# An encoder kernel in split float32: the up projection of three FFNs in groups of seven block products, and part of the weight splitting handed to adding DMAs

## The chip, the cores and the metric

One core of a Trainium2 chip runs the whole program. The metric is device microseconds (us) of one execution; the time before is the median of 3 runs. A core has five engines that are used here. TensorE (PE in the profile) multiplies matrices, VectorE (DVE) and ScalarE (ACT) work elementwise, GpSimd (POOL) does little, and SyncE (SP) issues the DMAs that bring the weights. Each engine takes its instructions in a fixed order that a scheduler lays down when the kernel is built; they meet through semaphores.

## The reference

x has 256 tokens of 1024 features, everything is float32, and there are two layers. The part that matters here is the FFN, which stands twice in each layer, so four times in all:

```python
def swiglu(h, w_up, w_down):
    a, b = jnp.split(h @ w_up, 2, axis=-1)
    return (jax.nn.silu(a) * b) @ w_down

for l in range(DEPTH):
    h = rms_norm(x, ffn1_pre_g[l])
    x = x + 0.5 * rms_norm(swiglu(h, ffn1_w_up[l], ffn1_w_down[l]), ffn1_post_g[l])
    ...   # mixer: pooling, differential attention, cross-attention, gates, w_out
    h = rms_norm(x, ffn2_pre_g[l])
    x = x + 0.5 * rms_norm(swiglu(h, ffn2_w_up[l], ffn2_w_down[l]), ffn2_post_g[l])
```

w_up is 1024 x 5632 (2816 gate columns, then 2816 value columns), w_down is 2816 x 1024.

## The kernel before, in words

**Stages.** `stages` lists six in a row: FFN, mixer, FFN, FFN, mixer, FFN. Each ends with a sandwich norm (`post_norm`, then `pre_norm` of the next stage) for the two halves of 128 tokens, called c = 0 and c = 1. While the norm of c = 1 runs, PE already works on c = 0 of the next stage; the transposes of c = 1 (`late`) are placed behind the 37th matmul of that stage (`T_UP = 36`).

**Split float32.** A product of float32 operands is made of three matmuls in the PE's float32r format: high times high, high times low, low times high (`mm3`, L218). So each weight has to be split. Weights come in units of 1 MB (`raw`, 128 x 2048 float32), one DMA each from SP. `next_unit` (L105) splits a unit in two halves of 1024 columns (in four quarters for the first five units of a stage, `FINE`): ACT copies it, rounded, into `wh` (L116), DVE subtracts, raw - wh, into `wl` (L117). The pools hold 3 `raw` tiles and 5 pairs of `wh` and `wl`, and so the splitting runs at most five units ahead of PE.

**The up projection.** A pair p is 256 gate and 256 value columns with all 1024 rows of w_up, two units; an FFN has 11 pairs. In the first FFN, and for pairs 0 and 1 of the later three, `form_b2` (L253) makes a bank of 128 tokens by 512 columns for each c: 24 matmuls of 512 columns. `swiglu` (L327) takes the silu on ACT (L335) and the product on DVE (L336); `turn` (L338) transposes the 128 x 256 result on PE (L341) and splits it into `hid` (L156, L157). For pairs 2 to 10 of the later three FFNs, `up2` (L347) uses `form_a2` (L235), with the weights as the stationary operand: for each bank eight matmuls of 512 and eight of 256 columns, whose result stands already transposed; ACT and DVE add the parts (L356, L357), take silu and product (L358, L359), and split.

**The down projection.** `down(p)` (L298) splits one unit of w_down, 256 rows, and adds it into four accumulator banks, 24 matmuls of 512 columns (`rows_chunk`, L256). Down units 0 to 7 stand between the pairs, two behind; units 8 to 10 are done in `tail`.

**What sets the order.** The order of the program text, a pool's free buffers and the scheduler set the order on each engine; a few positions are pinned by hand (`issue_after`). PE's order follows the text closely. DVE and ACT serve two kinds of work from one queue: splits of units that come later, and what the current banks need (evictions, norms, splits of hid).

Of the kernel before, what the change touches and what calls it, by code (L numbers as in the profile page):

```python
# [35 lines left out]
T_SC = (242, 336)  # L36
T_KT = (200, 222)
# [10 lines left out]
def encoder_kernel(ctx, tc, x_d, xt_d, mem_d, memt_d, pos_d, w_d, gains_d, cols_d, lamv_d, poolw_d, cst_d, out_d):  # L48
# [4 lines left out]
    rawp = ctx.enter_context(tc.tile_pool(name="rawp", bufs=3))  # L53
# [3 lines left out]
    mixp = ctx.enter_context(tc.tile_pool(name="mixp", bufs=1))  # L57
    s4 = ctx.enter_context(tc.tile_pool(name="s4", bufs=2))
    s2 = ctx.enter_context(tc.tile_pool(name="s2", bufs=5))
# [45 lines left out]
    def next_unit():  # L105
        parts = 4 if fine[0] > 0 else 2
        fine[0] -= 1
        if not raws:
            load_unit()
        raw = raws.pop(0)  # L110
# [3 lines left out]
        for s in range(parts):  # L114
            cs = slice(s * n, (s + 1) * n)
            high = nc.scalar.copy(out=h[:, cs], in_=raw[:, cs])  # L116
            low = nc.vector.tensor_tensor(out=l[:, cs], in0=raw[:, cs], in1=h.bitcast(F32)[:, cs], op=ALU.subtract)  # L117
# [4 lines left out]
        return h, l  # L122

# [19 lines left out]
    def rstd_of(halves, fold=1.0, between=None, into=None, listed=False):  # L143
        s, sq = sm(2), []
        for i, h in enumerate(halves):
            junk = small.tile([P, 512], BF16, name="junk", bufs=2)
# [32 lines left out]
    def pre_norm(c, src, g, xx):  # L179
# [13 lines left out]
        def turn():  # L193
            tps = []
            for b in range(2):
# [5 lines left out]
                split(pv, xh[:, c, b * 4:b * 4 + 4, :], xl[:, c, b * 4:b * 4 + 4, :])  # L201
            return tps
# [83 lines left out]
    def ffn(i, xx, late, g_post, finish, ahead, raw_rstd=None):  # L286
# [4 lines left out]
        def hid_pair(p):  # L291
            hid[p] = (hids.tile([P, 2, 2, P], F32R, name="hid"), hids.tile([P, 2, 2, P], F32R, name="hid"))
            return hid[p]

        def lhs_of(c, kk, k):
            return hid[kk][0][:, c, k, :], hid[kk][1][:, c, k, :]

        def down(p):  # L298
            w = next_unit()
# [3 lines left out]
            for c in range(2):  # L303
                rows_chunk(c, acc[c], [(w, p)], lhs_of, 0, NPR - 1)

        pending = []

        def flush():
            while pending:
                pending.pop(0)()  # L310
# [7 lines left out]

        def up_first(p, ws):
            banks = [ma_bank(), ma_bank()]  # L320
            for i, w in enumerate(ws):
                for c in range(2):
                    mm3(banks[c], half_b(w, i, c, xx), i == 0, i == 1)
# [3 lines left out]
        def swiglu(p, c, ps):  # L327
            sg = t2((P, 2, P))
            gate, value = (ps[:, 256 * j:256 * j + 256].rearrange("p (u m) -> p u m", u=2) for j in range(2))
            hn = t2((P, 2, P))  # L330
            if raw_rstd:
# [601 lines left out]
```

## Time and profile before

| what | value |
|---|---|
| median of 3 runs | 1139.08 us (1138.89 to 1139.74) |
| the profiled execution | 1138.92 us, its span 1136.9 us |
| PE busy | 1127.8 us |
| DVE busy | 749.6 us |
| ACT busy | 626.8 us |
| POOL busy | 25.6 us |
| bytes moved by DMA | 218.32 MB |

The span runs from the first to the last instruction of the profiled execution. A busy share is that of an engine's instructions with matmul ends modelled: successive matmuls overlap in it. The mean duration of a matmul is therefore longer than the step from one to the next, and the step is what counts for a row of matmuls. The same holds, less strongly, for DVE and ACT. The chain of waits goes back from the last instruction to whatever released it, and gives the stretches of the program in order of time. The three later FFNs lie at 384 to 570, 570 to 756 and 946 to 1137 us of the span.

### The profile page before, as it was taken

Reading aid. Unit: us, or ns where it says so; the run is one execution under the profiler, and the core shown is the slowest. Engines: PE = TensorE matmul, PEld = TensorE weight load, DVE = VectorE, ACT = ScalarE, POOL = GpSimd, SP = SyncE. Lnnn points to the kernel's source line nnn. Section 1 sums busy time; section 2 is a strip of 40 time slices with the busy share of each in tenths; the row PEclk is TensorE's granted clock in tenths of the full one; section 3 lists DMA queues with packets and bytes.
Section 4 is the critical chain, followed back from the end, with each engine's and each line's share of the span. In section 5 each row is a group of like instructions: output and inputs, shape, how many; then the busy total and the mean of one; then the engine's idle time right before and its main releaser. Section 6 shows DMA issues by size and latency. Waiting matters only on the chain.

```text
span 1136.9 us, 14731 instructions
## 1 busy us (share of the span) xinstructions
PE 1127.8 (99%) x5679; PEld 943.7 (83%) x5679; DVE 749.6 (66%) x1164; ACT 626.8 (55%) x1121; POOL 25.6 (2%) x37
## 2 busy tenths in 40 slices
PE   9999999999999999999999999999999999999997
PEld 6888888888788888888888888888887888888886
DVE  6767456567758866566586756575676688666553
ACT  7666445456573565555565655555566546555541
POOL 0000000000000100000000000010000001000000
PEclk9999999999999999999999999999999999999999
DMA  8976553544554575555465655545455545655530
GB/s 318 340 239 229 194 189 131 213 171 148 205 183 168 204 256 192 186 185 186 148 238 206 222 189 184 186 158 204 161 180 184 203 148 177 249 185 185 186 111 37
DMA packets 35493, 218.32 MB, mean 192 GB/s; under 512 B 4192, under 2 KB 4448, under 8 KB 11232
## 3 DMA queue, kind: packets, MB, share of 16 engines
q1 hardware_dynamic: 35424, 217.40, 53.4%
q8 instruction: 44, 0.72, 0.2%
q14 instruction: 25, 0.20, 0.1%
HBM read 216.33 MB, written 1.05 MB: 191 GB/s over the span
## 4 chain that ended last, share of the span: by engine, by line
PE 97%; DMA 1%; ACT 1%; DVE 0%; POOL 0%; issue 0%; SPq 0%; DVEq 0%; POOLq 0%; ACTq 0%
PE ma L224 36%; PE acc L266 25%; PE mb L243 13%; PE ma L243 13%; PE mb L224 2%; PE acc L224 2%; PE mb L199 1%; PE acc L599 1%; PE mb L341 1%; PE acc L622 1%; PE mb L497 1%; PE acc L685 1%; DMA hid<-in_xt 1%; DMA raw<-in_w 0%; PE acc L669 0%; PE mb L758 0%
## 5 line engine op out<-in xcount | busy, mean ns | idle before, releaser
L117 DVE TENSOR_TENSOR wl<-raw,wh 128x1024 fp32r<-128x1024 f32 (+1 forms) x444 | 459.0, 1075 | 150.8 <-ACT wh L116 145.0
L116 ACT CAST wh<-raw 128x1024 fp32r<-128x1024 f32 (+1 forms) x444 | 391.3, 935 | 187.8 <-issue 99.9
L224 PE MATMUL ma<-wh,xhl 128*128 128x512 f32 x1184 | 376.6, 393 | 0.8 <-ACT wh L116 0.8
L224 PEld LDWEIGHTS ma<-wh,xhl 128*128 128x128 f32 x1184 | 221.4, 188 | 47.5 <-ACT wh L116 1.7
L224 PE MATMUL ma<-wl,xhl 128*128 128x512 f32 x592 | 233.6, 395 | 0.2 <-DVE wl L117 0.2
L266 PE MATMUL acc<-wh,hid 128*128 128x512 f32 x704 | 224.6, 391 | 0.0
L243 PE MATMUL ma<-xhl,wh 128*128 128x512 f32 x432 | 157.4, 398 | 0.0
L243 PE MATMUL mb<-xhl,wh 128*128 128x512 f32 x432 | 157.0, 397 | 0.0
L266 PEld LDWEIGHTS acc<-wh,hid 128*128 128x128 f32 x704 | 132.2, 188 | 26.2
L266 PE MATMUL acc<-wl,hid 128*128 128x512 f32 x352 | 137.1, 389 | 0.0
L224 PEld LDWEIGHTS ma<-wl,xhl 128*128 128x128 f32 x592 | 111.3, 188 | 23.9 <-DVE wl L117 1.2
L243 PE MATMUL mb<-xhl,wl 128*128 128x256 f32 x432 | 112.5, 281 | 0.0
L243 PE MATMUL ma<-xhl,wl 128*128 128x256 f32 x432 | 112.4, 281 | 0.0
L243 PEld LDWEIGHTS ma<-xhl,wh 128*128 128x128 f32 x432 | 81.2, 188 | 15.8
L243 PEld LDWEIGHTS mb<-xhl,wh 128*128 128x128 f32 x432 | 81.5, 189 | 14.5
L357 DVE TENSOR_TENSOR s<-mb,s 128x256 f32<-128x256 f32 x54 | 22.9, 424 | 103.8 <-ACT s L356 103.8
L243 PEld LDWEIGHTS mb<-xhl,wl 128*128 128x128 f32 x432 | 81.6, 189 | 5.0
L243 PEld LDWEIGHTS ma<-xhl,wl 128*128 128x128 f32 x432 | 81.5, 189 | 4.6
L266 PEld LDWEIGHTS acc<-wl,hid 128*128 128x128 f32 x352 | 66.2, 188 | 13.7
L356 ACT COPY s<-mb 128x256 f32<-128x256 f32 x54 | 20.2, 373 | 58.7 <-PE mb L243 58.7
L358 ACT ACTIVATE s<-s 128x256 f32<-128x256 f32 x54 | 22.6, 418 | 50.6 <-DVE s L357 50.6
L140 POOL TENSOR_TENSOR sm<-sm,mhalf 128x1 f32<-128x1 f32 (+1 forms) x26 | 22.6, 869 | 1024.5 <-DVE sm L149 845.6
(162 smaller groups left out, 966.0 us busy)
## 6 DMA issues: line engine op xcount, KB each, us to landing
raw<-in_w SPq DMA_DIRECT2D x189, 1024.0 KB, 4.8
gain<-in_gains SPq DMA_DIRECT2D x17, 512.0 KB, 5.1
raw<-in_w SPq DMA_DIRECT2D x8, 256.0 KB, 5.7
hid<-in_memt SPq DMA_DIRECT2D x8, 256.0 KB, 6.0
hid<-in_xt SPq DMA_DIRECT2D x4, 256.0 KB, 5.6
raw<-in_w SPq DMA_DIRECT2D x2, 512.0 KB, 6.9
x<-in_x SPq DMA_DIRECT2D x4, 256.0 KB, 6.6
hid<-in_mem SPq DMA_DIRECT2D x4, 256.0 KB, 6.1
```

What stands on the lines that cost most here:

```text
L116: high = nc.scalar.copy(out=h[:, cs], in_=raw[:, cs])
L117: low = nc.vector.tensor_tensor(out=l[:, cs], in0=raw[:, cs], in1=h.bitcast(F32)[:, cs], op=ALU.subtract)
L140: nc.gpsimd.tensor_tensor(out=r, in0=v, in1=mhalf[:, :n], op=ALU.pow)
L199: tps.append(nc.tensor.transpose(out=ps[:, k * P:(k + 1) * P], in_=xn[:, i * P:(i + 1) * P], identity=ident))
L224: done.append(nc.tensor.matmul(out=out, lhsT=lhsT, rhs=rhs, start=(first and i == 0), stop=(last and i == n - 1)))
L243: nc.tensor.matmul(out=o, lhsT=ww[:, k, ms], rhs=rhs, start=(k == 0 and o is full), stop=(k == KT - 1 and o is full))
L266: done.append(nc.tensor.matmul(out=banks[b], lhsT=a, rhs=ww[:, k, fs], start=(kk == first and k == 0 and i == 0), stop=(kk == last and k = ...
L341: nc.tensor.transpose(out=tp[:, u * P:(u + 1) * P], in_=hn[:, u, :], identity=ident)
L356: nc.scalar.copy(out=half, in_=banks[i][:, S:2 * S])
L357: nc.vector.tensor_tensor(out=half, in0=banks[i][:, 0:S], in1=half, op=ALU.add)
L358: nc.scalar.activation(out=t[:, 0:S], in_=t[:, 0:S], func=AF.Silu)
L497: ins.append(nc.tensor.transpose(out=tp[:, i * P:(i + 1) * P], in_=a[:, hh, kt * P:(kt + 1) * P], identity=ident))
```

## The change

**Seven products for eight.** In the later three FFNs, six of the 11 pairs are done two at a time. The 256 x 1024 input is seen as 2 x 2 blocks (c, and the halves of the 1024 features), the 1024 x 1024 piece of w_up of two pairs as 2 x 2 blocks (the same halves, and 512 gate or 512 value columns), one raw unit for each block. `group` makes the four result blocks of seven products of blocks, 12 matmuls of 512 columns each, in place of eight. To that end it adds raw units to each other on DVE before they are split (four additions of 128 x 2048 in a group), uses four sums of token blocks (`token_sums`, once in an FFN, from unsplit copies that `pre_norm` keeps with four ACT copies), and puts the products together with seven DVE additions of 128 x 512. The first group of an FFN (`s0`) also does pair 0 in the ordinary way, around the late transposes; pairs 1 and 2 are its group. The other groups (`g5`, `g9`) do pairs 5, 6 and 9, 10. Pairs 3, 4, 7 and 8 go by `form_b2`, so `form_a2` and `up2` are gone. `PLAN` is the order.

**Down units 0 to 7** of these FFNs get their low part without DVE: ACT writes -wh into `wl` (line 121 of the new kernel), and a DMA issued by POOL adds raw to it in memory (line 122), two halves of 512 KB a unit.

**Buffers.** 5 `raw` tiles for 3, 8 `s2` tiles for 5, one `junk` tile for two; the mixer's tiles `vc`, `up`, `pooled` and `pw` live in one raw tile. In all FFNs the transposes of a pair now are made in `down`, behind its c = 0 and c = 1 parts.

```diff
+PLAN = [[(t[0], int(t[1:])) for t in plan.split()] for plan in (
+    "u2 d0 u3 d1 u4 d2 u5 d3 u6 d4 u7 d5 u8 d6 u9 d7 u10",
+    "s0 d0 u3 d1 u4 d2 g5 d3 d4 u7 d5 u8 d6 g9 d7",
+)]
...
-    rawp = ctx.enter_context(tc.tile_pool(name="rawp", bufs=3))
+    rawp = ctx.enter_context(tc.tile_pool(name="rawp", bufs=5))
...
             high = nc.scalar.copy(out=h[:, cs], in_=raw[:, cs])
+            if added:
+                nc.scalar.activation(out=l[:, cs], in_=h.bitcast(F32)[:, cs], func=AF.Copy, scale=-1.0)
+                nc.gpsimd.dma_start(out=l[:, cs], in_=raw.bitcast(F32R)[:, cs], accum_op=ALU.add)
+                continue
             low = nc.vector.tensor_tensor(out=l[:, cs], in0=raw[:, cs], in1=h.bitcast(F32)[:, cs], op=ALU.subtract)
...
+                if keep is not None:
+                    keep[c, b] = t2()
+                    nc.scalar.copy(out=keep[c, b], in_=ps)
...
         def down(p):
-            w = next_unit()
+            w = split_unit(next_raw(), 2, True) if kept else next_unit()
...
             for c in range(2):
                 rows_chunk(c, acc[c], [(w, p)], lhs_of, 0, NPR - 1)
+                flush(1 - c)
...
+        def token_sums():
+            a11, a12, a21, a22 = (kept[c, b] for c in range(2) for b in range(2))
+            s1 = t2()
+            nc.vector.tensor_tensor(out=s1, in0=a22, in1=a21, op=ALU.subtract)
+            nc.vector.tensor_tensor(out=a21, in0=a11, in1=a21, op=ALU.subtract)
+            nc.vector.scalar_tensor_tensor(out=a11, in0=s1, scalar=-1.0, in1=a11, op0=ALU.mult, op1=ALU.subtract)
+            nc.vector.scalar_tensor_tensor(out=a12, in0=a11, scalar=-1.0, in1=a12, op0=ALU.mult, op1=ALU.subtract)
+            for j, t in enumerate((s1, a11, a21, a12)):
+                split(t.rearrange("p (k t) -> p k t", t=P), sums[:, 0, 4 * j:4 * j + 4, :], sums[:, 1, 4 * j:4 * j + 4, :])
+
+        def group(p, start):
+            def turn(c, value, gate):
+                nc.scalar.activation(out=gate, in_=gate, func=AF.Silu)
+                nc.vector.scalar_tensor_tensor(out=value, in0=value, scalar=-1.0, in1=gate, op0=ALU.mult, op1=ALU.mult)
+                turned(value, c, [p, p + 1])
+
+            if start:
+                ws = (next_unit(), next_unit())
+                done = up(p, 0, ws, acc_bank)
+                w11, w21 = next_raw(), next_raw()
+                a, e = ma_bank(), ma_bank()
+                done += product(a, tokens(0, 0), split_unit(w11, 2))
+                done += product(e, tokens(0, 1), split_unit(w21, 2))
+                issue_after(late, done[T_UP])
+                s, g0 = t2(), t2()
+                nc.scalar.copy(out=s, in_=a)
+                add(g0, s, e)
+                up(p, 1, ws, acc_bank)
+                p += 1
+                token_sums()
+                w12, w22 = next_raw(), next_raw()
+            else:
+                w11, w12, w22, w21 = (next_raw() for _ in range(4))
+                a = ma_bank()
+                product(a, tokens(0, 0), split_unit(w11, 2))
+                flush()
+                s = t2()
+                nc.scalar.copy(out=s, in_=a)
+            add(w11, w11, w12)
+            d = mb_bank()
+            product(d, summed(0), split_unit(w11, 2))
+            flush()
+            add(w11, w11, w22)
+            add(w12, w12, w22)
+            b = mb_bank()
+            product(b, summed(1), split_unit(w11, 2))
+            u2, u3 = t2(), t2()
+            add(u2, s, b)
+            c = ma_bank()
+            product(c, summed(2), split_unit(w12, 2))
+            add(u3, u2, c)
+            add(u2, u2, d)
+            if not start:
+                e, g0 = ma_bank(), s
+                product(e, tokens(0, 1), split_unit(w21, 2))
+                add(g0, s, e)
+            v1 = t2()
+            add(v1, u3, d)
+            add(w21, w21, w11)
+            g = ma_bank()
+            if start:
+                product(g, tokens(1, 1), split_unit(w21, 2))
+                add(u3, u3, g)
+                turn(1, v1, u3)
+            f = mb_bank()
+            product(f, summed(3), split_unit(w22, 2))
+            add(u2, u2, f)
+            turn(0, u2, g0)
+            if not start:
+                product(g, tokens(1, 1), split_unit(w21, 2))
+                add(u3, u3, g)
+                turn(1, v1, u3)
```

**How the instructions move.** First place: DVE at the start of the second FFN (384 us of the span before), from the scaling of c = 1 in the norm on. Before, there are splits of units (`wl`), the split of the late transposes (`xhl`), the swiglu products (L336) and splits of `hid`:

```order
L191 TENSOR_SCALAR s4_3305<-s4_3305,sm_3315 128x512 x2
L117 TENSOR_TENSOR wl_3374<-raw_3371,wh_3373 128x512 x3
L336 TENSOR_TENSOR s2_3413<-ma_3387,s2_3412 128x256
L117 TENSOR_TENSOR wl_3523<-raw_3520,wh_3522 128x512 x2
L157 TENSOR_TENSOR xhl_3209<-mb_3319,xhl_3209 128x512
L157 TENSOR_TENSOR xhl_3209<-mb_3326,xhl_3209 128x512
L117 TENSOR_TENSOR wl_3523<-raw_3520,wh_3522 128x512 x2
L336 TENSOR_TENSOR s2_3447<-ma_3416,s2_3446 128x256
L157 TENSOR_TENSOR hid_3384<-mb_3441,hid_3383 128x256
```

Now, at the same place (line numbers are those of the new kernel: L124 is the split of a unit, L368 an addition, L345 the swiglu product, L169 any other split, L379 to L382 the token sums, with the splits of the sums among them):

```order
L203 TENSOR_SCALAR s4_3303<-s4_3303,sm_3313 128x512 x2
L124 TENSOR_TENSOR wl_3416<-raw_3393,wh_3415 128x1024
L368 TENSOR_TENSOR raw_3391<-raw_3391,raw_3486 128x2048
L169 TENSOR_TENSOR xhl_3203<-mb_3317,xhl_3203 128x512
L169 TENSOR_TENSOR xhl_3203<-mb_3326,xhl_3203 128x512
L124 TENSOR_TENSOR wl_3493<-raw_3391,wh_3492 128x1024
L345 TENSOR_TENSOR s2_3388<-acc_3362,s2_3387 128x256
L368 TENSOR_TENSOR raw_3486<-raw_3486,raw_3488 128x2048
L368 TENSOR_TENSOR s2_3434<-s2_3433,ma_3396 128x512
L124 TENSOR_TENSOR wl_3493<-raw_3391,wh_3492 128x1024
L345 TENSOR_TENSOR s2_3470<-acc_3437,s2_3469 128x256
L169 TENSOR_TENSOR hid_3466<-mb_3462,hid_3465 128x256
```

The additions of whole raw units stand in front of the split of the late transposes and among the evictions of pair 0; the four sums and their splits follow, then the splits of the four remaining products. From the row behind the scaling to the second half of the last product's `wl`, DVE now has 34 instructions: 11 half-unit splits, 4 additions of 2048 columns, 13 additions, subtractions or splits of 512, 2 fused ones of 512 and 4 of 256 columns.

Second place: ACT at the end of that first group. The casts of the last two products (`wh_3564`, `wh_3586`) stand in front of down unit 0 (`wh_3609`) and its negation:

```order
L119 CAST wh_3540<-raw_3486 128x1024
L119 CAST wh_3564<-raw_3393 128x1024 x2
L119 CAST wh_3586<-raw_3488 128x1024 x2
L119 CAST wh_3609<-raw_3607 128x1024 x2
L121 ACTIVATE wl_3610<-wh_3609 128x1024 x2
L388 ACTIVATE s2_3537<-s2_3537 128x512
```

POOL's queue, which held only the norms' square roots there, now has the two additions of each of the eight down units between those of one stage's end and the next:

```order
L152 TENSOR_TENSOR sm_3299<-sm_3295,mhalf_90 128x1
L152 TENSOR_TENSOR sm_3313<-sm_3309,mhalf_90 128x1
L122 DMA wl_3610<-raw_3607 128x1024 x2
L122 DMA wl_3759<-raw_3756 128x1024 x2
L122 DMA wl_3883<-raw_3880 128x1024 x2
```

So the low part of a down unit now goes raw, ACT, ACT, POOL, DMA, PE, where it went raw, ACT, DVE, PE.

More of the change, by code (lines that the diff above doesn't have):

```diff
@@ L819, in ahead @@
                     nx["mem"] = mem_gain(l)
-            late = ffn(i, cur, late, gain(l * 10 + row + 1), finish, ahead, [rst[:, c:c + 1] for c in range(2)] if i == 0 else None)
+            late = ffn(i, cur, late, kept, gain(l * 10 + row + 1), finish, ahead, [rst[:, c:c + 1] for c in range(2)] if i == 0 else None)
         else:
             late = mix(l, cur, late, mem, finish)
-        cur, mem = nx.get("xx"), nx.get("mem")
+        cur, mem, kept = nx.get("xx"), nx.get("mem"), nx.get("kept")
 def _constants(np):
```

179 lines of the change are left out of this document (93 added, 86 removed).

## The prediction

> **What bounds the kernel now.** I read the page first, then the chain of waits in order of time, then busy time by stage, then the groups with shapes kept apart, and last the timelines of single engines at a stage boundary. The page's engine table, its row of the granted clock, and the chain's shares:
>
> ```profile
> PE 1127.8 (99%) x5679; PEld 943.7 (83%) x5679; DVE 749.6 (66%) x1164; ACT 626.8 (55%) x1121; POOL 25.6 (2%) x37
> PEclk9999999999999999999999999999999999999999
> PE 97%; DMA 1%; ACT 1%; DVE 0%; POOL 0%; issue 0%; SPq 0%; DVEq 0%; POOLq 0%; ACTq 0%
> ```
>
> The chain runs through PE for 97% of the span, so PE's own work sets the time, and less of it is worth something as long as nobody else becomes late. The three later FFNs, by stage (window, length, then busy us and count of PE, PEld, DVE, ACT, POOL, then clock, DMA share, GB/s):
>
> ```profile
> 384.00:570.00 186.00, 186.00 (x962) 158.31 (x961) 120.92 (x181) 101.68 (x178) 3.50 (x4) 1.00 0.56 198
> 570.00:756.00 186.00, 186.00 (x962) 158.11 (x961) 123.51 (x189) 104.18 (x185) 3.43 (x4) 1.00 0.56 198
> ```
>
> PE has no gap there; DVE is busy 121 of 186 us (65%), so it has some 65 us to spare in an FFN, but spread over it. Steps come from the chain (start, length, engine, target, line, count), first in the first FFN, then in the second:
>
> ```profile
> 47.91 5.44 PE ma L224 x24
> 53.36 0.22 PE mb L341 x2
> 53.58 5.48 PE ma L224 x24
> 59.05 0.22 PE mb L341 x2
> 59.27 0.93 PE acc L266 x4
> ...
> 401.88 5.47 PE ma L224 x24
> ...
> 424.51 2.81 PE ma L243 x16
> 427.32 2.82 PE mb L243 x16
> 430.14 2.82 PE ma L243 x16
> 432.96 2.82 PE mb L243 x16
> 435.78 5.45 PE acc L266 x24
> 441.23 2.81 PE ma L243 x16
> ```
>
> 24 matmuls of 512 columns take 5.47 us, 0.228 each, and two transposes 0.22. A pair by `form_b2` with its four transposes takes 59.27 - 47.91 = 11.36 us; a pair by `form_a2` 435.78 - 424.51 = 11.27; a down unit 5.45.
>
> **What PE saves.** A group of two pairs is 7 x 12 = 84 matmuls and 8 transposes: 84 x 0.228 + 4 x 0.22 = 20.0 us. Before, an FFN's up projection is 2 x 11.36 + 9 x 11.27 = 124.2 us; after, 5 x 11.36 + 3 x 20.0 = 116.8. That is 7.4 us an FFN, 22.2 for three: seven products for eight give 2.7 us a group, and the pairs 3, 4, 7 and 8 lose 0.1 each. Against the profiled execution's 1138.9 us, PE's work alone would give 1116.7.
>
> **What DVE gets.** Durations by shape (mean ns after the comma) and, from DVE's timeline, steps between instructions that stand back to back:
>
> ```profile
> L117 DVE TENSOR_TENSOR wl<-raw,wh 128x1024 fp32r<-128x1024 f32 x324 | 383.0, 1220 | 139.9 <-ACT wh L116 134.3 <-issue 1.1 <-PE ma L224 0.4
> L752 DVE TENSOR_TENSOR hid<-hid 128x512 f32<-128x512 f32 x8 | 5.5, 686 | 0.1
> ```
> ```profile
> 380.84 4.29 DVE L117 TENSOR_TENSOR wl<-raw,wh 128x512 fp32r<-128x512 f32 x7
> 385.06 0.20 DVE L149 TENSOR_SCALAR sm<-sm 128x1 f32<-128x1 f32 x1
> 385.92 1.41 DVE L216 SCALAR_TENSOR_TENSOR x<-s,sm,x 128x512 f32<-128x512 f32 x2
> 390.31 0.88 DVE L191 TENSOR_SCALAR s<-s,sm 128x512 f32<-128x512 f32 x2 [0.45 <-POOL sm L140]
> 400.06 2.36 DVE L117 TENSOR_TENSOR wl<-raw,wh 128x1024 fp32r<-128x1024 f32 x2 [2.47 <-ACT wh L116]
> 402.34 0.42 DVE L336 TENSOR_TENSOR s<-ma,s 128x256 f32<-128x256 f32 x1
> 402.68 0.41 DVE L157 TENSOR_TENSOR hid<-mb,hid 128x256 fp32r<-128x256 f32 x1
> ```
>
> Steps: 1024 columns 2.36 - 1.22 = 1.14 us; 512 columns (4.29 - 0.69) / 6 = 0.60; a fused one of 512 1.41 - 0.75 = 0.66; 256 columns 402.68 - 402.34 = 0.34. No row has 2048 columns: going on from 512 to 1024 (0.54 per 512) gives 2.2, four pieces of 512 give 2.4, and a gain cannot be excluded from these rows, since two TENSOR_SCALARs of 512, at 390.31, take 0.88. I take 2.2, nearest to the two-input rows.
>
> The first group `s0` is the place where it decides. From the scaling of c = 1 to the second half of the last product's `wl`, DVE's queue holds (front, the order) 11 x 1.14 + 4 x 2.2 + 13 x 0.60 + 2 x 0.66 + 4 x 0.34 = 31.8 us. It cannot be begun earlier, since the queue is in order and the scaling ends the norm's chain; the unit buffers, five ahead of PE, are nearly all taken then. PE's rows at that place before:
>
> ```profile
> 384.03 0.39 PE L224 MATMUL ma<-wh,xhl 128*128 128x512 f32 x1
> 392.42 1.04 PE L199 MATMUL mb<-ident,s 128*128 128x128 f32 x8
> 393.21 0.48 PE L224 MATMUL ma<-wl,xhl 128*128 128x512 f32 x1
> ```
>
> Call 384.03 zero. The scaling ends at 7.2 (390.31 + 0.88), the late transposes start at 8.4 and take 0.8. Behind them PE has 11 matmuls (rest of product e), 24 (pair 0, c = 1), five products of 12, and 4 transposes: 95 x 0.228 + 0.8 + 0.44 = 22.9 us, so it would end the group at 31.3. DVE is done with the last `wl` at 7.2 + 31.8 = 39.0 at the earliest, and six matmuls (1.4) stand behind: 40.4. PE waits 9.1 us. Two things come on top: two half splits of product a, and the gain of one bank, now stand ahead of c = 1's variance in place of three quarters (2 x 1.14 + 0.60 - 3 x 0.60 = 1.1, 1.0 taken), and DVE waits about 0.4 for the cast that follows the first addition (0.95, below). **10.5 us a start group**, 31.5 for three, between 8.5 (the second one has a split less behind the scaling) and 12.3 (additions at 2.4, and 1 us of more such waits). PE waits where DVE's order puts it: before product d (the token sum s1 comes behind the additions and the evictions of pair 0), and before g and f.
>
> In `g5` and `g9` the splits run ahead of PE by up to five units, with little else on DVE during the pairs before. What stays behind the preceding down unit's end is the cast for e, then e, 2.28, a hid split 0.34, an addition 2.2, f 2.28, half of g 1.14, u2 0.60, the rest of g 1.14, u3, u2, v1 1.8: 11.8 + 1.2 for the cast (0.95 by the row below, and the handing over) = 13.0 us, when product f gets its bank; PE is through a, d, b, c, e at 13.7. No wait, with 0.7 us of cover; without it, each 0.5 us of more work on DVE costs six times 0.5.
>
> **Down units by an adding DMA.** DVE loses 2.3 us for each, ACT gains two negations. ACT's and the DMAs' rows (KB each, median us to landing in the second fence):
>
> ```profile
> 402.24 2.01 ACT L116 CAST wh<-raw 128x1024 fp32r<-128x1024 f32 x2
> ```
> ```profile
> raw<-in_w SPq DMA_DIRECT2D x189, 1024.0 KB, 4.8
> raw<-in_w SPq DMA_DIRECT2D x2, 512.0 KB, 6.9
> out<-x SPq DMA_DIRECT2D x4, 256.0 KB, 2.1
> ```
>
> ACT's step is 2.01 - 1.05 = 0.95 us. Unit 0 stands on ACT behind the casts of g and f. The addition that g needs ends on DVE about 25.5 into the queue, at 34.1; four casts, two of unit 0 and one negation are 6.7 us, so the first DMA is issued at 40.8. PE ends f at 41.8 and has four matmuls of unit 0, four transposes and three matmuls of pair 3 before it needs that half: 43.8. So 3.0 us are covered. An adding DMA from POOL is not in the trace; 256 KB land in 2.1 us, 512 KB in 6.9 at the crowded start, so PE waits between 0 and 3.9. I take 4.5, between them, since the 1 MB loads take 4.8 amid traffic: 1.5 us a start group, **4.5 for three**. For units 3 and 7, behind `g5` and `g9`, the buffer comes free with product b; PE then has four products (10.9 us), ACT takes 2.9 to the first negation: 8.0 us are covered. The other units have a pair's 11 us in front of them.
>
> The Trainium skill's page "DMA: Bandwidth & Descriptors" (section "Anatomy of one DMA — SWDGE (gpsimd) path") fits a DMA from this queue as 2.0 us plus bytes over 436 GB/s: an estimate of 3.2 us for 512 KB, by which unit 0 would wait 0.2 us and the time be 4 us lower. No run here shows it, and it is fitted for plain copies.
>
> **Edits at nothing.** The four copies that `pre_norm` keeps (0.5 us each on ACT) lie beside DVE's queue, which is later; if ACT were the later one, 1 us per boundary. Raw tiles are held longer in a group, and SP's loads queue behind one another: unit 4's load goes out when w21's addition has read w11, 4.8 us before ACT wants it; the next units' loads behind it have a pair's time. The moved `flush`, the shared `junk` and the mixer's tiles in a raw slot sit in stages where PE has no wait now, and the loads run three units ahead.
>
> **The sum.** 1138.9 - 22.2 + 31.5 + 4.5 = 1152.7 us. The profiled execution lies 0.2 us below the median of the runs, which is nothing here; what the measurement tells from no change is about 0.2%, 2.3 us.
>
> **Rivals.**
> *The start groups wait less than they save (faster).* If additions between two SBUF tiles of 2048 columns stepped twice as fast as the splits, a start group would lose 4 x 1.1 = 4.4 us of DVE's queue, PE would wait 6.1, and with the DMA covered the time would be 1138.9 - 22.2 + 18.3 = 1135.0. For it: the one-input row at 390.31. Against: two-input rows of SBUF (L752) cost what those with a PSUM operand or a cast cost. It decides where an FFN's waits sum to less than 7.4 us. 0.10.
> *They cancel.* Waits of 6.6 to 8.2 us an FFN: 1136.6 to 1141.3. 0.05.
> *The adding DMA is slow.* From 8 us to landing on, units 3 and 7 come late too. At 9 us it is 4.5 more for unit 0 and 1 each for 3 and 7, 6.5 an FFN: 1172; at 12 us 15.5 an FFN: 1199. For it: it reads both addends and writes one, beside loads that hold the DMA engines 56% busy; against: nothing but the lengths above. 0.14.
> *PE's clock falls in the waits.* Before product g PE has only a matmul or two in some 4 us. If the next product then ran at half speed, 2.7 us a start group: 1160.8. The granted clock is 1.00 in every window of the trace, but so is PE without gaps. 0.08. The page "TensorE: Matmul & The Clock Gate" (Part 1) states that rule: after an idle window of 3.4 us the array runs at half its clock until it has been busy for as long. By it the price is an estimate of 1.7 us; the few matmuls in between would prevent it.
>
> **The numbers.** The forecast, PE waiting on DVE in the start groups, has 0.63, with 1138.9 - 22.2 + 26.2 = 1143 (waits of 9.1, 8.0 and 9.1, DMA covered) to 1138.9 - 22.2 + 36.9 + 11.7 = 1165 us as its own range. Faster 0.10, within 0.2% 0.05, slower 0.63 + 0.14 + 0.08 = 0.85. The range runs from 1141 to 1172: it leaves out the faster case, the cancelling one, and the worse part of the slow DMA, some 0.2 together.
>
> **What would show it.** In the profile after: stages of the later FFNs about 190 us long instead of 186; gaps of PE in the 25 us behind the late transposes, 9 to 12 us in each FFN, released by DVE's `wl` and sums; DVE without a pause there; no gaps inside `g5` and `g9`; in front of down unit 0 a short wait for a DMA. Wrong it would be if DVE's 2048-column additions take well under 2.2 us, if PE waits at other places, above all for DMAs in front of units 3 and 7, or if the FFNs come out shorter than 186 us.

## The result, and the profile after

The change made the kernel slower: 1198.16 us (median of 4 runs, 1196.80 to 1199.78) against 1138.99 (4 runs, 1138.57 to 1139.74), a ratio of 1.0519 with a 95% interval of 1.0501 to 1.0538, or 59 us. The prediction said 1152.7 us, with a range of 1141 to 1172: the sign was right, the size four times too small.

From the page after: the engines, the granted clock over the span, and the chain's shares.

```profile
PE 1134.9 (95%) x5247; PEld 922.8 (77%) x5247; DVE 842.8 (70%) x1167; ACT 698.8 (58%) x1130; POOL 68.6 (6%) x85
...
PEclk9999999999999889999888999999999998899999
...
PE 34%; DMA 5%; DVE 4%; issue 3%; ACT 2%; POOL 1%; POOLq 0%; DVEq 0%; ACTq 0%
```

The chain after is followed back only to 604 us, so its shares add up to 49% of the span. Of these the DMA, DVE, ACT, POOL and the engines' own issue have 15, where PE had 97 of 100 before; and the granted clock falls below full speed in three places, one in each later FFN. The stages show where the time went. Here are windows from the first transposes of c = 0 of one stage to those of the next (window, length, busy us and count of PE, PEld, DVE, ACT, POOL, then clock, DMA share, GB/s): the three later FFNs.

```profile
379.57:592.99 213.42, 194.06 (x829) 155.06 (x829) 154.49 (x186) 127.40 (x186) 17.72 (x20) 0.94 0.67 212
592.99:795.23 202.24, 185.74 (x818) 150.42 (x817) 154.54 (x192) 127.85 (x189) 18.13 (x20) 0.96 0.70 219
...
983.28:1196.80 213.52, 191.92 (x838) 154.62 (x837) 150.57 (x178) 122.00 (x175) 17.07 (x20) 0.96 0.58 180
```

Cut at the same transposes (L199 in the kernel before, L211 after), the stages compare as follows, in us of the profiled executions; the other columns are kernels of the next section.

| stage | before | after | DVE splits the down units | no groups, no adding DMA | last kernel |
|---|---|---|---|---|---|
| first mixer | 186.9 | 188.1 | 188.0 | 188.1 | 188.0 |
| second FFN | 188.6 | 213.4 | 194.1 | 189.7 | 184.2 |
| third FFN | 186.0 | 202.2 | 189.1 | 188.7 | 182.9 |
| second mixer | 187.0 | 188.1 | 188.1 | 187.6 | 188.0 |
| last FFN, to the end | 197.0 | 213.5 | 202.3 | 198.1 | 192.6 |

The three later FFNs carry 57.6 of the 59.9 us between the two spans, the mixers about 1.1 each.

PE's rows with a wait in the second FFN (start, us, engine, line, operation, tiles, shape, count, idle time before it and its releaser) show two kinds:

```profile
405.89 0.79 PE L239 MATMUL mb<-wh,xhl 128*128 128x512 f32 x1 [2.49 <-ACT xhl L168]
408.65 1.22 PE L239 MATMUL mb<-wh,xhl 128*128 128x512 f32 x2 [1.11 <-DVE xhl L169]
420.75 0.50 PE L239 MATMUL ma<-wh,xhl 128*128 128x512 f32 x1 [2.20 <-ACT wh L119]
422.64 0.80 PE L239 MATMUL mb<-wh,xhl 128*128 128x512 f32 x1 [1.39 <-ACT wh L119]
434.94 0.50 PE L281 MATMUL acc<-wl,hid 128*128 128x512 f32 x1 [3.16 <-DMA wl<-raw]
...
495.96 0.50 PE L281 MATMUL acc<-wl,hid 128*128 128x512 f32 x1 [0.57 <-DMA wl<-raw]
498.41 0.50 PE L281 MATMUL acc<-wl,hid 128*128 128x512 f32 x1 [1.49 <-DMA wl<-raw]
...
570.32 0.80 PE L281 MATMUL acc<-wl,hid 128*128 128x512 f32 x1 [2.41 <-DMA wl<-raw]
```

The first four are the start group: product d waits for the token sum s1 (high, then low part), products g and f for casts that stand on ACT behind the last sum of weights, at the places that the prediction named. The others stand in front of down units, at a matmul that reads a half of `wl` for the first time: units 0, 3 and 7 in this FFN, with shorter waits of 0.56 and 0.95 us before units 1 and 4. In the third and the last FFN they stand before units 0 and 3 (and 1.26 us before unit 1 in the last), and not before unit 7. The waits put them in one row (total us, times, longest); beside it what held SP's queue of weight loads:

```profile
PE acc L281 <- DMA wl<-raw: 28.6, 17, 3.6
```
```profile
SPq L104 <- DMA wl<-raw: 221.4, 23, 15.5
```

So PE idles 28.6 us for the adding DMA. In the start groups the idle times sum to 7.3 us in each FFN, 22.1 us in all. And SP often cannot issue a load because a raw tile is still being read by an adding DMA. At an FFN's start it is the start group's own additions and splits that hold the tiles. SP's queue and windows of 12 us behind the second FFN's start show what that does to the transfers:

```profile
416.84 50.44 SPq L104 DMA_DIRECT2D raw<-in_w  x11
```
```profile
396.00:408.00 12.00, 8.89 (x36) 6.34 (x34) 11.97 (x14) 5.94 (x12) 0.00 (x0) 0.90 0.00 0
408.00:420.00 12.00, 9.90 (x34) 7.47 (x34) 11.75 (x14) 5.64 (x8) 0.00 (x0) 0.82 0.17 57
420.00:432.00 12.00, 9.65 (x35) 7.34 (x35) 9.65 (x14) 10.40 (x15) 1.97 (x2) 0.86 0.90 307
432.00:444.00 12.00, 8.62 (x33) 6.55 (x34) 5.15 (x10) 6.93 (x13) 0.97 (x2) 0.86 0.82 191
```

While the start group holds the raw tiles, no weights come (0 GB/s from 396 to 408, and SP's next load goes out at 416.84); then they come in a bunch, and in the midst of it POOL issues the first adding DMAs:

```profile
426.72 1.97 POOL L122 DMA_DIRECT2D wl<-raw  x2 [33.78 <-ACT wl L121]
```

The first of the two is what PE waits for at 434.94: 8.2 us from issue to landing. The last rows of this section show the clock: the steps of PE behind the second wait of unit 7.

```profile
570.91 1.05 PE L281 MATMUL acc<-wh,hid 128*128 128x512 f32 x2
571.77 0.63 PE L281 MATMUL acc<-wl,hid 128*128 128x512 f32 x1
...
576.35 0.39 PE L281 MATMUL acc<-wl,hid 128*128 128x512 f32 x1
576.58 0.61 PE L281 MATMUL acc<-wh,hid 128*128 128x512 f32 x2
```

Two matmuls from 570.91 take 571.77 - 570.91 = 0.86 us, 0.43 each in place of 0.23; from 576.35 the step is 576.58 - 576.35 = 0.23 again. Such slow stretches last 3 to 7 us behind a wait; here, over the two waits of unit 7, PE was slow from 566.26 to 576.35, and the granted clock of the window from 566 to 574 is 0.50.

### The profile page after: what moved, and what is told of

Read it like the earlier page. It is cut to its first block, busy times and chain, and to the rows that moved or that the text cites. A ratio compares the mean times of both kernels' runs of the same rounds, so it can differ in the third digit from the quotient of the medians.

```text
span 1196.8 us, 14046 instructions
## 1 busy us (share of the span) xinstructions
PE 1134.9 (95%) x5247; PEld 922.8 (77%) x5247; DVE 842.8 (70%) x1167; ACT 698.8 (58%) x1130; POOL 68.6 (6%) x85
## 5 line engine op out<-in xcount | busy, mean ns | idle before, releaser
L119 ACT CAST wh<-raw 128x1024 fp32r<-128x1024 f32 (+1 forms) x498 | 446.6, 947 | 222.0 <-PE ma L239 64.6
L124 DVE TENSOR_TENSOR wl<-raw,wh 128x1024 fp32r<-128x1024 f32 (+1 forms) x450 | 468.3, 1077 | 127.6 <-ACT wh L119 123.2
L239 PE MATMUL ma<-wh,xhl 128*128 128x512 f32 x1664 | 531.9, 394 | 4.4 <-ACT wh L119 4.4
L239 PEld LDWEIGHTS ma<-wh,xhl 128*128 128x128 f32 x1664 | 312.7, 189 | 71.0 <-ACT wh L119 6.3
L239 PE MATMUL ma<-wl,xhl 128*128 128x512 f32 x832 | 328.5, 395 | 0.2 <-DVE wl L124 0.2
L281 PE MATMUL acc<-wl,hid 128*128 128x512 f32 x352 | 143.4, 408 | 28.6 <-DMA wl<-raw 28.6
L239 PE MATMUL mb<-wh,xhl 128*128 128x512 f32 x280 | 96.4, 411 | 17.5 <-ACT xhl L168 11.8
L368 DVE TENSOR_TENSOR raw<-raw 128x2048 f32<-128x2048 f32 x36 | 82.3, 2287 | 9.6 <-DMA raw<-in_w 9.2
L239 PEld LDWEIGHTS mb<-wh,xhl 128*128 128x128 f32 x280 | 55.0, 198 | 31.5 <-ACT xhl L168 12.5
L169 DVE TENSOR_TENSOR hid<-mb,hid 128x256 fp32r<-128x256 f32 x88 | 36.9, 419 | 49.9 <-ACT hid L168 49.7
L239 PE MATMUL mb<-wl,xhl 128*128 128x512 f32 x140 | 56.9, 406 | 0.0
L239 PE MATMUL acc<-wh,xhl 128*128 128x512 f32 x160 | 52.4, 393 | 0.3 <-DVE xhl L169 0.3
L121 ACT ACTIVATE wl<-wh 128x1024 fp32r<-128x1024 f32 x48 | 49.6, 1054 | 0.1
L281 PE MATMUL acc<-wh,xhl 128*128 128x512 f32 x128 | 40.7, 394 | 0.0
```

Of the source, the lines that this page charges most:

```text
L121: nc.scalar.activation(out=l[:, cs], in_=h.bitcast(F32)[:, cs], func=AF.Copy, scale=-1.0)
L169: return high, nc.vector.tensor_tensor(out=l, in0=ps, in1=h.bitcast(F32), op=ALU.subtract)
L239: done.append(nc.tensor.matmul(out=out, lhsT=lhsT, rhs=rhs, start=(first and i == 0), stop=(last and i == n - 1)))
L281: done.append(nc.tensor.matmul(out=banks[b], lhsT=a, rhs=ww[:, k, fs], start=(kk == first and k == 0 and i == 0), stop=(kk == last and k = ...
L368: nc.vector.tensor_tensor(out=out, in0=a, in1=b, op=ALU.add)
```

## The experiments

**Theories.** A: two losses, each a wait of PE with slow matmuls behind it: the start groups, where DVE's queue is late, and the adding DMA directly behind a group, where it is issued late and lands late. B: the waits for the DMA are only the place where DVE's lateness comes out. C: the adding DMA costs wherever it runs, through the loads it crowds and the raw tiles it holds.

**1. The adding DMA undone (three groups stay).**

```diff
-            w = split_unit(next_raw(), 2, True) if kept else next_unit()
+            w = split_unit(next_raw(), 2) if kept else next_unit()
```

> All three groups stay; the down units get their low part from DVE again, as before the change. Theory A (read from the trace after): PE loses some 34 us in the start groups, behind DVE's queue, and some 45 us at the adding DMAs, which land in 9.9 us; both with the half-speed matmuls that follow a wait. Without the adding DMA the 45 us go, and unit 0's 2.3 us of splitting come back into DVE's late queue in three start groups: 1198 - 45 + 7 = 1160 us, between 1153 and 1168. Theory B: the waits for the DMA only show where DVE's lateness comes out; the adding DMA takes 18 us an FFN off DVE, and without it PE waits as long for DVE: 1190 us or more. By the steps of the prediction (4.5 us for the DMA): not under 1190 either, since the missing 45 us would lie elsewhere.

1154.85 us, 1.0133 (1.0118 to 1.0148) of before. The adding DMA costs 1198.16 - 1154.85 = 43.3 us, as A has it; B is out. PE's waits of the second FFN are now those of the start group alone:

```profile
406.06 0.50 PE L239 MATMUL mb<-wh,xhl 128*128 128x512 f32 x1 [2.51 <-ACT xhl L168]
408.82 1.22 PE L239 MATMUL mb<-wh,xhl 128*128 128x512 f32 x2 [1.41 <-DVE xhl L169]
420.61 0.50 PE L239 MATMUL ma<-wh,xhl 128*128 128x512 f32 x1 [1.70 <-ACT wh L119]
422.51 0.50 PE L239 MATMUL mb<-wh,xhl 128*128 128x512 f32 x1 [1.39 <-ACT wh L119]
```

**2. The adding DMA alone, without groups.** The plan of the later FFNs becomes that of before, all pairs by `form_b2`:

```diff
-    "s0 d0 u3 d1 u4 d2 g5 d3 d4 u7 d5 u8 d6 g9 d7",
+    "f0 u2 d0 u3 d1 u4 d2 u5 d3 u6 d4 u7 d5 u8 d6 u9 d7 u10",   # f0: pairs 0 and 1
...
```

The four copies that `pre_norm` keeps and the token sums, now without use, are left out too.

> No groups: all eleven pairs of the later FFNs in eight block products each, in the order of before; down units 0 to 7 get their low part by the adding DMA. Theory A: what hurts is that a group hands its buffers over late; in the old order a unit's buffer comes free some four units, 22 us, ahead of its use, and 2.9 us of ACT and 9.9 us of DMA fit into that: the same time as with neither change, 1141 us, within 0.3%. Theory C: the adding DMA costs wherever it runs, since it crowds the weight loads and holds the raw tiles: waits of 1 us or more in front of most of 24 units, with slow matmuls behind them, 1165 us or more.

**3. Neither.** Edits 1 and 2 together: no groups, and DVE splits the down units.

> No groups and no adding DMA; what is left of the change is form_b2 for all pairs, the transposes inside the down units and the larger pools. All theories: nine pairs an FFN cost 0.09 us more each, 2.4 us in all, and nothing waits: 1138.9 + 2.4 = 1141 us, within 0.3%.

The second took 1145.95 us, the third 1146.21, ratios of 1.0056 (1.0041 to 1.0071) and 1.0057 (1.0040 to 1.0073). Here the DMAs are issued well ahead of their use (unit 0 of the second FFN at 406.59, first read at 420.08; unit 1 at 420.35 and 436.92, so 13 to 17 us), and the adding DMA costs nothing; C is out as a general cost. It also lands sooner there. First the kernel after, then experiment 2:

```profile
DMA to landing us min/median/max: 4.6/9.9/14.0
```
```profile
DMA to landing us min/median/max: 4.5/6.0/7.4
```

What missed is the level: 1141 was expected of both. Some 4 us of the change lie in the edits that the prediction put at nothing (the table of stages has about 1 us in each mixer, and 2.7 in the third FFN, where 0.8 were counted for `form_b2`). For the mixers the traces show the place, transposes that wait for a norm's product on DVE. First before, then experiment 3:

```profile
PE mb L639 <- DVE s L635: 0.3, 2, 0.2
```
```profile
PE mb L725 <- DVE s L721: 2.5, 4, 0.6
```

The four squares that this norm takes on ACT all write a `junk` tile. With two such tiles they start 0.25 us apart (290.68, 290.93, 291.18 before), with one 0.40 (293.11, 293.51, 293.91 in experiment 3). So the shared `junk` is the likely cause of these 2.2 us; it was not tried by itself. Another 1.1 us is a wait at the end of the third FFN, for the scaling in the norm; its cause stays open.

**4. No start group, DVE splits the down units.**

```diff
-    "s0 d0 u3 d1 u4 d2 g5 d3 d4 u7 d5 u8 d6 g9 d7",
+    "f0 u2 d0 u3 d1 u4 d2 g5 d3 d4 u7 d5 u8 d6 g9 d7",   # token_sums() behind f0
...
```

> Pairs 0, 1 and 2 in eight products each, as before; the groups of pairs 5, 6 and 9, 10 stay, with their token sums; the down units on DVE. PE's own work: 7 pairs of 11.36 and two groups of 20.0 are 119.5 us an FFN for 124.2, 14 us less in three. Theory A: without the start group nothing puts DVE 32 us behind, and a group in the middle of the FFN finds its splits done ahead: 1138.9 - 14 = 1125 us, up to 1133 if the cover of 0.7 us in a group is short by 0.5 us in each product. Theory B (DVE is the bound of any group once it also splits the down units): 1145 us or more.

1137.71 us, 0.9985 (0.9976 to 0.9994): faster than before by a hair, but 13 us above A's number and between the ranges of A and B. No wait stands in a group; there is a new one at each FFN's start, followed up in 5, 12 and 13.

**5. The token sums later** (behind pair 3 instead of pair 1).

> As the kernel without a start group (groups of pairs 5, 6 and 9, 10, down units on DVE), but the token sums stand behind pair 3 in place of pair 1. There PE waited 2.1 us (1.3 in the second of the later FFNs) at the start of each FFN for a sum of pair 1 that stands behind the token sums on DVE, with 1.5 to 3.2 us of slow matmuls behind it. If DVE's order at the start is the cause (theory A), these 3 to 5 us an FFN go: 1137.7 - 12 = 1126 us, 1123 to 1130. If DVE is short of time in the FFN as a whole (theory B), the wait comes back later: 1134 us or more.

1137.48 us, 0.9980 (0.9972 to 0.9989). The sums were not the cause; the wait stays as it was, at pair 0's first transposes:

```profile
399.44 0.41 PE L329 MATMUL mb<-ident,s 128*128 128x128 f32 x2 [1.95 <-DVE s L345]
```

**6. PE kept busy in the start group.** On the kernel of experiment 1, with `zr` a zero tile:

```diff
+        def idle(out, n):
+            for j in range(n):
+                nc.tensor.matmul(out=out, lhsT=zr, rhs=xx[0][:, 0, 0:4, :], start=(j == 0), stop=False)
...
```

> The kernel with all three groups and the down units on DVE; before three products of the start group PE gets matmuls with a zero stationary operand that add nothing to the bank: 20 before d, 14 before g (in every group), 6 before f, in all 40 x 0.228 = 9 us, about as long as PE waits there. Theory of the clock (PE's matmuls run at half speed for some us behind a wait): the steps behind the waits stay 0.23 us instead of 0.43; behind the last wait of a start group that is 1.3 to 3 us, which are gained, while the slow ones between two waits for DVE are only turned into a longer wait; but the 14 in the other two groups cost 3.2 us each, 19 us in three FFNs, where PE does not wait: 1154.9 - 6 + 19 = 1168 us, granted clock back to 0.995 or more. If the slow steps come from something else than the wait: 1174 us or more, and the granted clock stays at 0.988.

The expectation describes the kernel wrongly: the 14 before g stand only in the start group, so 40 are added to each FFN and the 19 us for the other groups drop out. Put right, the theory of the clock gives 1154.9 - 6 = 1149 us at best. Measured: 1155.63 us, against 1154.85 without the edit. The granted clock is 0.999 in place of 0.988 and the slow steps are gone, so they do come from the waits:

```profile
403.40 4.92 PE L369 MATMUL mb<-xhl,zr 128*128 128x512 f32 x20
...
412.21 0.50 PE L242 MATMUL mb<-wl,xhl 128*128 128x512 f32 x1 [0.46 <-DVE wl L124]
```

But nothing was gained. That fits a start group in which PE's pace is DVE's: whether PE walks slowly or stands still between two results of DVE is the same. The run does not settle it alone, since the 120 zero matmuls take 120 x 0.228 = 27 us, more than the 22 us that PE stands idle in the start groups of experiment 1, and may have used up the small gain behind the last waits.

**7. The start group without its four weight additions** (on experiment 1; the four `add` of raw tiles are skipped if `start`).

> All three groups and the down units on DVE, but the four additions of weight blocks in the start group are left out, so that its products are made of the wrong blocks: 4 x 2.2 = 8.8 us less in DVE's queue, and the same work for PE, ACT and DMA. If DVE's queue sets the waits of the start group, these 8 to 9 us of waits an FFN and the slow matmuls behind them go: between 1154.9 - 3 x 12 = 1119 and 1154.9 - 3 x 8.8 = 1128 us. If they come from the weights' arrival or from ACT, less than 9 us are gained in all: 1146 us or more.

1143.55 us: 11.3 gained, where DVE's queue as the only cause asked for 27 at least. The wait moved forward. DVE's order now lets more splits pass ahead of the token sum s1 (seven half units behind the scaling of c = 1, three in experiment 1), whose subtraction starts at 406.30 (404.68 in experiment 1), and product d waits for its cast:

```profile
406.30 0.69 DVE L379 TENSOR_TENSOR s<-s,s 128x512 f32<-128x512 f32 x1
```
```profile
407.69 0.50 PE L239 MATMUL mb<-wh,xhl 128*128 128x512 f32 x1 [3.75 <-ACT xhl L168]
```

DVE had one pause of 0.26 us between the scaling and this. It is still DVE's queue, but its order counts beside its length.

**8. More loads beside the adding DMA** (on experiment 2).

```diff
+        if twice[0]:
+            nc.sync.dma_start(out=raw[:, 0:1024], in_=w_d[nxt[0]][:, 0:1024])
...
```

> The kernel with adding DMAs and no groups, in which from the second FFN on the first half of each weight unit is loaded a second time: half as many bytes again for the loads, nothing else changed. If the adding DMA lands late because loads run beside it (it took 6.0 us in this order, where the DMA engines are half busy, and 9.9 in the groups, where they are 80 to 100% busy), its median goes to 8 us or more, and the time stays within 0.5% of 1146 us, since 20 us of cover hide it. If the groups make it late in another way (POOL's queue, two DMAs at once): it stays at 6.0 to 6.5 us.

The landing went as expected, from 6.0 to 10.6 us:

```profile
DMA to landing us min/median/max: 5.4/10.6/14.4
```
```profile
ACT wh L122 <- DMA raw<-in_w: 187.9, 40, 10.0
```

So loads alone, without any group, make it as late as it is after. The time did not go as expected: 1191.31 us, because the weights themselves now came late (the second row). PE waited for an adding DMA only once, 1.0 us: the cover of 13 to 17 us hides a landing of 10.6.

The kernel after holds the same comparison within itself. Unit 7 stands behind group g9 in each later FFN, but what is still to be loaded differs. Here are the landings of its two DMAs in the second and in the last FFN, and the packets, MB and share of the load queue from the first issue to the last landing (556.2 to 570.3, 1159.9 to 1167.1):

```profile
DMA to landing us min/median/max: 10.0/11.6/13.2
q1 hardware_dynamic: 351, 2.48, 47.8%
```
```profile
DMA to landing us min/median/max: 4.6/5.4/6.2
q1 hardware_dynamic: 65, 0.40, 13.8%
```

In the second FFN PE waits 4.9 us for them, in the last not at all. The third FFN is like the last: 0.73 MB of loads, 4.7 and 6.8 us to landing, no wait. The group ahead is the same; the loads beside the DMA are not.

**9. Two groups, no start group, adding DMAs** (experiment 5 with the down units as after).

> Two groups an FFN and no start group, with the adding DMA for units 0 to 7. Theory A (the adding DMA is late behind a group, whether or not DVE is): units 0 and 1 have 20 us of cover, units 3, 4 and 7 behind a group do not, and PE waits for them as it does after, with slow matmuls behind: 4 to 8 us an FFN on the 1137.5 us of the same kernel with DVE splitting, 1150 to 1162 us. If only the start group's lateness makes the DMA show, and the 18 us that DVE is spared do no more than before: 1137.5 us, within 3 us.

1166.73 us, 29 above experiment 5. The waits stand in front of unit 3 in all three FFNs and of unit 7 in the second, with no start group ahead of them; these are the second FFN's:

```profile
485.16 0.80 PE L281 MATMUL acc<-wl,hid 128*128 128x512 f32 x1 [3.57 <-DMA wl<-raw]
487.63 0.80 PE L281 MATMUL acc<-wl,hid 128*128 128x512 f32 x1 [0.82 <-DMA wl<-raw]
555.84 0.79 PE L281 MATMUL acc<-wl,hid 128*128 128x512 f32 x1 [2.51 <-DMA wl<-raw]
559.90 0.79 PE L281 MATMUL acc<-wl,hid 128*128 128x512 f32 x1 [2.41 <-DMA wl<-raw]
```

This is A, with a price above its range of 1150 to 1162.

**10 and 11. The adding DMA for units 0, 3 and 7 only, and for the other five only** (on the kernel after).

```diff
-            w = split_unit(next_raw(), 2, True) if kept else next_unit()
+            w = split_unit(next_raw(), 2, p in (0, 3, 7)) if kept else next_unit()
```

> All three groups; the adding DMA only for units 0, 3 and 7, which stand directly behind a group; DVE splits the other five. Theory A: the 43 us that the adding DMA costs come from these three: 1154.9 + 30 to 43 = 1185 to 1198 us. Theory C (every adding DMA costs its share, by what it takes from the loads and the time it holds a raw tile): 3/8 of 43: 1171 us, within 5.

> The complement: all three groups, the adding DMA for units 1, 2, 4, 5 and 6, DVE for units 0, 3 and 7. Theory A: four of the five have a pair's 11 us in front of them, unit 4 another down unit's 5.5: 1155 us, within 7. Theory C: 5/8 of 43 us: 1182 us, within 7.

Units 0, 3 and 7: 1204.60 us, 1.0582 (1.0563 to 1.0600), more than with all eight and 7 above A's range. The other five: 1166.77 us, 1.0245 (1.0231 to 1.0259), 12 above experiment 1 and 5 above A's range. C's two numbers, 1171 and 1182, are missed by 34 and 15. PE's waits for the DMA, first of 10, then of 11:

```profile
PE acc L281 <- DMA wl<-raw: 34.7, 12, 5.5
```
```profile
PE acc L281 <- DMA wl<-raw: 7.8, 4, 3.1
```

Place decides, and an equal share per DMA (C) is out: three units behind a group cost 50 us, five others 12. PE's waits of 11 all stand in front of unit 1, the first to come by DMA behind the start group. In 10 no two units' DMAs run at a time, and they still take 8.9 us in the median and up to 12.9, so crowding by another unit's adding DMAs is not needed for it. The two costs do not add up to the 43 of all eight; why fewer DMAs cost more in 10 was not followed further.

**12. The kept copies on POOL** (experiment 5, with `xh + xl` added by POOL in place of ACT's copy).

> Two groups an FFN (pairs 5, 6 and 9, 10), down units on DVE, sums behind pair 3; the four copies for the token sums are no longer made by ACT from PSUM, but by POOL, which adds the split parts again in SBUF. In the kernel without this edit PE waits 2.1, 1.3 and 2.1 us for the first pair's silu product, and the silu stands on ACT behind two of these copies, which wait for DVE; 1.5 to 3.2 us of slow matmuls follow. If the copies are the cause, both go: 1137.5 - 10 = 1127.5 us, 1125 to 1131. If the casts and splits of the late transposes hold the silu anyway: 1134 us or more.

1141.59 us, 4 slower than experiment 5. The wait at pair 0's transposes is still there, 2.64 us in place of 1.95. Taking the copies off ACT does not remove it.

**13. Pair 0's first transposes one pair later** (experiment 5; banks of c = 1 of pairs 0 and 1 from the accumulators' pool).

```diff
+            flush(leave)          # in up(); 1 for pair 1, c = 0, of the start
-                        done += up(q, c, ws[q])
+                        done += up(q, c, ws[q], acc_bank if c else ma_bank, 1 if (q, c) == (1, 0) else 0)
...
```

> Two groups an FFN, down units on DVE, sums behind pair 3, copies on ACT again; pair 0's first transposes stand one pair later, and the banks of c = 1 of pairs 0 and 1 come from the accumulators' pool, so that PE neither needs the silu product of pair 0 nor its bank until 5.5 us later. If the wait at the start is a matter of place alone, the 2.1, 1.3 and 2.1 us go, and the slow matmuls behind them (1.5 to 3.2 us): 1137.5 - 10 = 1127.5 us, 1125 to 1131. If ACT and DVE are behind by more than 5.5 us there: 1134 us or more.

1130.48 us, 0.9921 (0.9908 to 0.9935) of before: the one version that beats both kernels clearly, by 8.8 us. The wait is gone, and the later FFNs come out near what PE's count said, 4.4, 3.1 and 4.4 us shorter than before for 4.7 each; the second of them keeps a wait of 1.1 us at its end:

```profile
380.26:564.48 184.22, 184.22 (x841) 152.05 (x841) 152.09 (x187) 107.46 (x166) 3.49 (x4) 1.00 0.55 200
564.48:747.40 182.92, 181.80 (x830) 149.74 (x829) 152.91 (x193) 108.41 (x169) 3.42 (x4) 1.00 0.53 192
```

PE is busy throughout the first and DVE 152 of 184 us: two groups an FFN fit beside DVE's splits, if nothing else is late.

## Why the prediction was wrong, by its own steps

The experiments measure each term but PE's saving, which is counted (medians; a pair by `form_b2` is 11.36 us, so eleven of them are 125.0, the count with three groups is 116.8, and it falls by 8.2 us an FFN from experiment 3 to 1, 24.5 in all):

| step | predicted | measured | from |
|---|---|---|---|
| `form_b2` for nine pairs, edits at nothing | +2.4 | +6.7 | experiment 3 - before |
| seven products for eight, against that | -24.5 | | PE's count |
| waits of the start groups | +31.5 | +33.1 | (experiment 1 - 3) + 24.5 |
| the adding DMA | +4.5 | +43.3 | after - experiment 1 |

- *What PE saves: right.* It is a count, and experiment 13, where little covers it, shows it nearly whole for two groups. (The 2.7 us a group of the text are against two pairs by `form_b2`; against the pairs that stood there before it is 2.5 to 2.6. The sum of 7.4 an FFN holds.)
- *Start groups: right in mechanism and size.* From experiment 3 to 1 the three FFNs lose 12.6, 8.6 and 12.4 us against PE's count, where 8.5 to 12.3 was the range for one. DVE's queue was reckoned at 31.8 us from the end of the scaling to the last half of `wl`; it took from 392.98 + 0.88 to 421.45 + 4.62, 32.2 us:

```profile
392.98 0.88 DVE L203 TENSOR_SCALAR s<-s,sm 128x512 f32<-128x512 f32 x2 [0.45 <-POOL sm L152]
...
405.10 2.29 DVE L368 TENSOR_TENSOR raw<-raw 128x2048 f32<-128x2048 f32 x1
407.30 0.69 DVE L380 TENSOR_TENSOR s<-s,s 128x512 f32<-128x512 f32 x1
...
421.45 4.62 DVE L124 TENSOR_TENSOR wl<-raw,wh 128x1024 fp32r<-128x1024 f32 x4
```

The addition of 2048 columns steps by 407.30 - 405.10 = 2.20 us, the value taken, so the faster rival falls. Of PE's loss 22.1 us are idle; the rest, by the trace, is mostly its slow steps.
- *Groups g5 and g9: right.* No wait stands inside them.
- *The adding DMA: this step failed.* "I take 4.5, between them, since the 1 MB loads take 4.8 amid traffic", and for units 3 and 7 "8.0 us are covered". The cover was about right: the half that unit 0 needs was issued at 426.72, 5.1 us before PE wanted it (434.94 - 3.16), where 3.0 were reckoned; unit 3's was issued at 487.63, 7.8 before, and unit 7's at 556.25, 7.6 before. The landing was not: 9.9 us in the median, up to 14.0, while 4.5 is less than the shortest of the 48, 4.6. In the prediction's own formula 9.9 gives waits of 6.9 for unit 0 and 1.9 each for units 3 and 7, 10.7 an FFN, 32 us. This is the rival *the adding DMA is slow*, which got 0.14; waits in front of units 3 and 7 are also what the prediction named as a sign against itself. That the result lies beside that rival's 1199 us is in part luck: 1199 is its time for 12 us, and at 9.9 it gives 1180. The formula is wrong in three things: the second half lands later still and is waited for by itself; unit 7 is waited for in one FFN only; and slow steps follow these waits with no DVE behind them to hide them. That last part, some 14 us, is 43.3 less the 28.6 of waiting; PE's busy time for the same 5247 matmuls, 1134.9 us after and 1119.4 in experiment 1, agrees. No run took it apart.
- *Edits at nothing: this step failed too.* "the next units' loads behind it have a pair's time". They did not. A start group holds the raw tiles, the loads stop (0 GB/s for 12 us) and return in a bunch, just when the first adding DMAs are issued. Experiment 8 shows that loads beside it are enough to bring the landing from 6.0 to 10.6 us, and unit 7 shows that behind the same group it is late with loads beside it and not late without. That holding the tiles is what brings those loads to that moment is read from the profiles, not tried by itself. And the stages "where PE has no wait now" had no time to spare: experiment 3 is 4.3 us above its count, 2.2 of them waits in the mixers.
- The Trainium skill's page "DMA: Bandwidth & Descriptors" (section "Anatomy of one DMA — SWDGE (gpsimd) path") gave an estimate of 3.2 us for 512 KB by its fit. The traces do not agree for an adding DMA: 4.5 us at the least, 6.0 and 9.9 in the median of two kernels. The measurement decides.
- *PE's clock falls in the waits: it does, but in the start groups keeping it up gained nothing* (experiment 6), against the 2.7 us a start group of that rival. Behind a wait for the DMA it does cost, by the 14 us above.

## What to carry to other kernels

A transfer put in place of an engine's work is priced by when its source and its buffer come free and by what else is in flight at that moment, not by a median of other transfers; the same adding DMA cost nothing with 13 to 17 us of cover and 43 us with groups ahead of it. Before holding tiles longer, look at which loads wait for them and when these will come instead. And once the engine that sets the pace has been found, the order of the queues around it can be worth as much as its length: moving two transposes by a pair and two banks to another pool gave 7 us, leaving out 26 us of additions gave 11.

## What the runs showed of the hardware that was not expected

- An adding DMA of 512 KB within SBUF landed in 4.5 to 7.4 us in one order of the work and in 4.6 to 14.0 in another; half as many load bytes again brought its median from 6.0 to 10.6. For one and the same unit it took 10.0 and 13.2 us beside 2.48 MB of loads and 4.6 and 6.2 beside 0.40 MB.
- PE's steps doubled from 0.23 to 0.43 us, for 3 to 7 us, behind most waits of 2.2 us and more and behind two of 1.6 and 1.5 us that stood 2.5 us apart (706.59 and 709.06, third FFN); behind 0.57 and 1.49 us as close together (495.96 and 498.41, second FFN) they did not. The length of the wait does not settle it: in experiment 5 a wait of 1.95 us was followed by a granted clock of 0.59 from 400 to 404 in the second FFN, and the same wait by 1.00 from 961 to 965 in the last. Matmuls on a zero operand that filled the waits kept the clock at 0.999. The Trainium skill's page "TensorE: Matmul & The Clock Gate" (Part 1) puts the fall after an idle window of some 3.4 us; the trace agrees with the halving, but not with that length, since most of these waits were shorter.

```profile
706.59 0.50 PE L281 MATMUL acc<-wl,hid 128*128 128x512 f32 x1 [1.63 <-DMA wl<-raw]
...
709.06 0.59 PE L281 MATMUL acc<-wl,hid 128*128 128x512 f32 x1 [1.51 <-DMA wl<-raw]
```
